# Cutting single matmuls of a split-precision product stream into 128-column pieces, and a last sub-layer in 256-column products

## The chip, the cores and the metric

The kernel runs on one core of one Trainium2 chip. The metric is the device time of one execution in microseconds; before the change it is 658.05 us, the median of three runs (657.58 to 658.54).

## What is computed

A two-layer decoder trunk on 256 tokens of width 1024, in float32. Layer 0 is a gated DeltaNet mixer followed by a squared-ReLU MLP, layer 1 a block attention (at 256 tokens it is plain causal softmax with ALiBi) followed by another such MLP. Every sub-layer is preceded by an RMSNorm, and one more stands at the end. Cut to what matters:

```python
for i in range(DEPTH):
    hn = rmsnorm(h, mix_norm_g[i])
    mix = gated_deltanet(hn, ...) if i % 2 == 0 else moba_layer(hn, ...)
    h = h + mix
    h = h + squared_relu_mlp(rmsnorm(h, mlp_norm_g[i]), mlp_w_up[i], mlp_w_down[i])
return rmsnorm(h, final_norm_g)
```

MLP: `square(relu(hn @ w_up)) @ w_down`, with 4096 hidden features.

## The kernel before

**Split products.** Each large weight product is made from three matmuls. A weight `w` and an activation `x` are each split into a high part and a rest (`wh`, `wl`, `xh`, `xl`, type fp32r), and `wh*xh + wh*xl + wl*xh` is summed in PSUM. `mm3` (lines 128 to 131) issues the three; the 128x128 weights are stationary and 256 tokens stream. In `natural` (lines 207 to 222) and in `mlp_last` the roles are turned: a 128x128 piece of the activation is stationary and up to 512 columns of weights stream. Every matmul brings its own load of the stationary side, so there are as many weight loads as matmuls. Below, a **split product** is one matmul of this kind; an **fp32 product** is a plain fp32 matmul or transpose (norm sums, attention scores, the recurrence).

**Weights.** They come as 200 units of 128x1024 from HBM in a fixed order. `unit()` hands out the next and prepares four ahead: SP issues the DMA, ScalarE makes `wh` (line 115), VectorE `wl` (line 116).

**Order of the work.** It is the program's order. Layer 0: the DeltaNet, in which split products of `pair` alternate with blocks of fp32 products by the hand-written string `ORDER`; `project_out("g")` (tiles `ps_g`, interleaved at its beginning with the last of the recurrence); MLP 0 in `mlp_up` (tiles `ps_up_m`, 16 calls of `pair`, 48 split products each) and `mlp` (`ps_dn_m`, 768). Layer 1: attention by the string `ATT` (tiles `ps_qk`, `ps_vn`, with fp32 blocks `s`, `ptp`, `pv` between), `project_out("a")` (`ps_a`, 192 split products), four transposes each for two token tiles (`hNt`), then `mlp_last`: 768 split products of `mlp_up` and the down product. The norm of an MLP is finished late: `nm.finish()` is called after the first `pair`, and issues four fp32 sums (`n_ps`) and two fp32 broadcasts (`n_pb`) among the split products of the first two pairs. Behind `n_pb` there is no fp32 product until the end of MLP 0 and the first pair of attention (`n_ps` of the next norm), and none until the end of the kernel in MLP 1.

**The last sub-layer.** `mlp_last` makes the down product in two halves of 512 output features. In each, for 8 groups of 4 hidden tiles and 2 token tiles `tt`, 12 split products run. Three of the four (half, tt) stream 512 columns into one PSUM bank, the last (half 1, tt 1) streams 256 columns at a time into two banks (`ps_last`, `ps_last_e`), so that the first 256 can be taken out earlier. `part`, `scaled` and `store` (lines 295 to 320) add, sum squares, scale and store.

Of the kernel before, what the change touches and what calls it, by code (L numbers as in the profile page):

```python
# [14 lines left out]
P = 128  # L15
T = 256
D = 1024
KT = D // P
H = 8
FF = 4 * D  # L20
NFF = FF // P
# [7 lines left out]
NLAST = 2  # L29
NTANH = 3  # L30
RS = 3.0 / 8
LASTCUT = 256
# [43 lines left out]
def trunk_kernel(ctx: ExitStack, tc: tile.TileContext, xT, wst, wba, par, con, selc, gfin, out):  # L76
    nc = tc.nc
# [8 lines left out]
    def bank(role, shape, name):  # L86
        tag = ROLE[role]
        return psum.tile(shape, F32, tag=tag, name=name, bufs=BANKS[tag])
# [32 lines left out]
    def unit():  # L121
        u = cur[0]
        cur[0] += 1
        for i in range(u, u + LEAD + 1):
            prep(i)
        return ring[u]

    def mm3(o, wh, wl, xh, xl, start, stop):
        nc.tensor.matmul(o, wh, xh, start=start, stop=False, skip_group_check=True)  # L129
        nc.tensor.matmul(o, wh, xl, start=False, stop=False, skip_group_check=True)  # L130
        nc.tensor.matmul(o, wl, xh, start=False, stop=stop, skip_group_check=True)  # L131

    def mm(o, l, r, start=True, stop=True):
        nc.tensor.matmul(o, l, r, start=start, stop=stop, skip_group_check=True)  # L134
# [56 lines left out]
            self.bc = small.tile([P, T], F32, tag="nbc", name=f"{self.name}_bc", bufs=2)  # L191
            nc.scalar.copy(self.bc, pb[:, :T])

    def pair(nm, name):

        ps = bank("acc", [P, 2, T], f"ps_{name}")
        for c in range(2):
            wh, wl = unit()
            for k in range(4):
                kt = 4 * c + k  # L200
                for n in range(2):
                    s = slice((k * 2 + n) * P, (k * 2 + n + 1) * P)
                    mm3(ps[:, n, :], wh[:, s], wl[:, s], nm.xh[:, kt, :], nm.xl[:, kt, :],
                        kt == 0 and n == 0, kt == KT - 1)
        return ps

    def natural(nm, name):
# [16 lines left out]
    def project_out(name, oh, ol, hin, nxt):  # L224

        pss = [bank("out" + "abcd"[i], [P, 2, T], f"ps_{name}_{i}") for i in range(4)]

        def piece(hd, n, w):
            s = slice(n * P, (n + 1) * P)
            mm3(pss[n // 2][:, n % 2, :], w[0][:, s], w[1][:, s], oh[:, hd, :], ol[:, hd, :],  # L230
                hd == 0 and n % 2 == 0, hd == H - 1)

        first = H - NLAST
        for hd in range(first):
            w = unit()
            for n in range(KT):
                piece(hd, n, w)
        w = [unit() for _ in range(first, H)]
        hout = act.tile([P, KT, T], F32, tag="h", name=f"h_{name}")
        for n in range(KT):  # L240
            for k in range(H - first):
                piece(first + k, n, w[k])
            if n % 2:
                i = n // 2
                nc.vector.tensor_add(hout[:, 2 * i:2 * i + 2, :], hin[:, 2 * i:2 * i + 2, :], pss[i])
                nxt.feed(hout, i)
        return hout

    def mlp_up(hp, name, nm):
        hp.tile([P, 336], F32, tag="fill", name=f"fill_{name}")  # L250
        hh = hp.tile([P, NFF, T], F32R, name=f"hh_{name}")
        hl = hp.tile([P, NFF, T], F32R, name=f"hl_{name}")
        for i in range(NFF // 2):
            ps = pair(nm, f"up_{name}_{i}")
            if i == 0:
                nm.finish()
            r1 = hp.tile([P, 2, T], F32, tag="r1", name=f"r1_{name}_{i}", bufs=2)
            nc.vector.scalar_tensor_tensor(r1, ps, 0.0, nm.bc[:, None, :].to_broadcast([P, 2, T]),
                                           op0=ALU.max, op1=ALU.mult)
            sq = hp.tile([P, 2, T], F32, tag="sq", name=f"sq_{name}_{i}", bufs=2)  # L260
            nc.scalar.activation(sq, r1, AF.Square)
            s = slice(2 * i, 2 * i + 2)
            nc.scalar.copy(hh[:, s, :], sq)
            nc.vector.tensor_sub(hl[:, s, :], sq, hh[:, s, :].bitcast(F32))
        return hh, hl
# [19 lines left out]
    def mlp_last(nm, hin):  # L285

        with tc.tile_pool(name="hid_last", bufs=1) as hp:
            hh, hl = mlp_up(hp, "m1", nm)
            gf = hp.tile([P, D], F32, name="gf")
            nc.sync.dma_start(gf, gfin)  # L290
            hg = hp.tile([P, 2, D], F32, name="hg")
            junk = hp.tile([P, 2, 512], F32, name="junk")
            ss = small.tile([P, 2, 3], F32, tag="ssf", name="ssf", bufs=1)

            def part(tt, a, b, k, o):

                f = slice(a, b)
                nc.vector.tensor_add(hin[:, tt, f], hin[:, tt, f], o)
                nc.scalar.activation(junk[:, tt, :b - a], hin[:, tt, f], AF.Square, accum_out=ss[:, tt, k:k + 1])

            def scaled(tt, a, b):
                nc.vector.scalar_tensor_tensor(hg[:, tt, a:b], hin[:, tt, a:b], RS, gf[:, a:b],
                                               op0=ALU.mult, op1=ALU.mult)

            def store(tt):
                so = small.tile([P, 1], F32, tag="sof", name=f"sof{tt}", bufs=2)
                if tt == 0:
                    nc.vector.tensor_scalar(so, ss[:, tt, 0:1], D * EPS, None, op0=ALU.add)
                else:
                    nc.vector.scalar_tensor_tensor(so, ss[:, tt, 0:1], D * EPS, ss[:, tt, 1:2],  # L310
                                                   op0=ALU.add, op1=ALU.add)
                ms = small.tile([P, 1], F32, tag="msf", name=f"msf{tt}", bufs=2)
                nc.vector.tensor_scalar(ms, ss[:, tt, 1 + tt:2 + tt], so, 1.0 / D, op0=ALU.add, op1=ALU.mult)
                r = rsqrt(ms, 1, f"fin{tt}")
                for a, b, q in ((0, DCUT, nc.sync), (DCUT, D, nc.scalar)):
                    if a == 0:
                        nc.vector.tensor_scalar(hg[:, tt, a:b], hg[:, tt, a:b], r, None, op0=ALU.mult)
                    else:
                        nc.scalar.activation(hg[:, tt, a:b], hg[:, tt, a:b], AF.Copy, scale=r)
                    q.dma_start(out[tt, :, a:b], hg[:, tt, a:b])  # L320

            for half in range(2):
                f0 = half * 512
                pss = [bank("acc", [P, 512], f"ps_last_{half}_{tt}") for tt in range(2)]
                pse = bank("pv0", [P, 512], f"ps_last_{half}_e")
                for c in range(0, NFF, 4):
                    w = [unit(), unit()]
                    for tt in range(2):
                        for a, b in ((0, LASTCUT), (LASTCUT, 512)) if half + tt == 2 else ((0, 512),):
                            o = pse[:, :b - a] if a else pss[tt][:, :b]  # L330
                            for k in range(4):
                                kt = c + k
                                wh, wl = w[k // 2]
                                s = slice(k % 2 * 512 + a, k % 2 * 512 + b)
                                xh, xl = hh[:, kt, tt * P:(tt + 1) * P], hl[:, kt, tt * P:(tt + 1) * P]
                                mm(o, xh, wh[:, s], kt == 0, False)
                                mm(o, xh, wl[:, s], False, False)
                                mm(o, xl, wh[:, s], False, kt == NFF - 1)
                            if c == NFF - 4:
                                part(tt, f0 + a, f0 + b, half + (a > 0), o)  # L340
                                scaled(tt, f0 + a, f0 + b)
                                if half == 1 and (tt == 0 or a):
                                    store(tt)
# [27 lines left out]
    with tc.tile_pool(name="gd", bufs=2) as gd:  # L371
# [349 lines left out]
        for tok in ORDER.split():  # L721
            c, n = tok[0], int(tok[1:] or 0)
# [33 lines left out]
        oh, ol = OH  # L756
        n1 = Norm("n1", G_MLP0)
        h1 = project_out("g", oh, ol, h0, n1)
    n2 = Norm("n2", G_MIX1)
    h2 = mlp("m0", n1, h1, n2)  # L760


    with tc.tile_pool(name="at", bufs=2) as at:
# [64 lines left out]
        for tok in ATT.split():  # L828
            {"q": do_qk, "s": do_soft, "t": do_pt, "V": do_vn, "p": do_pv}[tok[0]](int(tok[1:]))
        n3 = Norm("n3", G_MLP1)  # L830
        h3 = project_out("a", ah, al, h2, n3)
    hN = act.tile([P, 2, KT, P], F32, tag="h", name="hN")
    for tt in range(2):
# [124 lines left out]
```

## Time and profile before

| | |
|---|---|
| median of the runs | 658.05 us |
| the profiled execution | 658.23 us |
| its span, first to last instruction | 656.4 us |
| PE (TensorE matmul) busy | 643.4 us, 98% |
| PEld (weight load) busy | 605.2 us, 92% |
| DVE (VectorE), ACT (ScalarE) busy | 454.6 us (69%), 345.6 us (53%) |
| HBM read | 107.51 MB, 165 GB/s over the span |

Times are us from the start of the span. L130 is line 130 of the kernel. A matmul's shown duration is its latency: matmuls overlap in the array, so the time that one takes from the stream is the distance from its start to the next start, called its **pace** here.

### The profile page before, as it was taken

The page shows a single profiled execution, that of the slowest core. Times are in us where ns is not written, and L with a number is a line of the kernel's source. Part 1 is how long each engine was busy: PE and PEld are TensorE (multiplying, and loading weights), DVE is VectorE, ACT ScalarE, POOL GpSimd, SP SyncE. Part 2 cuts the span into 40 slices and gives each one's busy share as a digit, 9 for nine tenths or more (in the row PEclk, how much of TensorE's full clock was granted, in tenths as well). Part 3 has the DMA queues.
Part 4 walks back from the last instruction along what each step waited for, and adds up shares of the span by engine and source line. Part 5 has one row for each costly group of instructions (what it writes and reads, how often), then busy time and mean ns, then how long its engine had stood idle before and what let it go on. Part 6 is the DMA issues. An engine that isn't in the chain of part 4 may idle for free.

```text
span 656.4 us, 13349 instructions
## 1 busy us (share of the span) xinstructions
PE 643.4 (98%) x5454; PEld 605.2 (92%) x5454; DVE 454.6 (69%) x841; ACT 345.6 (53%) x570; POOL 4.0 (1%) x10
## 2 busy tenths in 40 slices
PE   8999999999999999999999999999999999999995
PEld 6999878979999999999999999889999999888994
DVE  5899998997897666645554668775976666545443
ACT  7689782553575555534443444543655555434331
POOL 1000000000000000000000000000000000000000
PEclk9999999999999999999999999999999999999998
DMA  8754151342555555565555555555365555556531
GB/s 268 240 171 154 36 192 68 103 126 65 187 168 193 187 176 189 187 193 190 179 182 190 184 169 161 165 157 170 119 224 191 185 178 190 171 188 186 190 129 65
DMA packets 32029, 109.42 MB, mean 167 GB/s; under 512 B 3552, under 2 KB 3936, under 8 KB 31968
## 3 DMA queue, kind: packets, MB, share of 16 engines
q1 hardware_dynamic: 31248, 107.71, 49.9%
q8 instruction: 43, 0.70, 0.4%
q10 hardware_dynamic: 720, 0.86, 0.4%
q14 instruction: 18, 0.15, 0.1%
HBM read 107.51 MB, written 1.05 MB: 165 GB/s over the span
## 4 chain that ended last, share of the span: by engine, by line
PE 86%; DVE 6%; DMA 4%; ACT 3%; issue 1%; DVEq 0%; ACTq 0%
PE ps_last L134 12%; PE ps_up_m L130 9%; PE ps_up_m L131 9%; PE ps_up_m L129 9%; PE ps_dn_m L130 5%; PE ps_dn_m L129 5%; PE ps_dn_m L131 5%; PE ps_vn L134 3%; DMA wf<-in_w 3%; PE ps_z L134 3%; DVE wl L116 2%; PE ps_qk L130 2%; PE ps_qk L131 2%; PE ps_qk L129 2%; PE kk L134 2%; PE ps_last_e L134 1%
## 5 line engine op out<-in xcount | busy, mean ns | idle before, releaser
L116 DVE TENSOR_TENSOR wl<-wf,wh 128x1024 fp32r<-128x1024 f32 (+1 forms) x208 | 244.8, 1182 | 144.9 <-ACT wh L115 144.5
L115 ACT CAST wh<-wf 128x1024 fp32r<-128x1024 f32 (+1 forms) x208 | 210.7, 1017 | 244.3 <-PE ps_up_m L130 65.4
L130 PE MATMUL ps_up_m<-n_l,wh 128*128 128x256 f32 x512 | 143.9, 281 | 0.2 <-DVE n_l L168 0.2
L131 PE MATMUL ps_up_m<-n_h,wl 128*128 128x256 f32 x512 | 144.0, 281 | 0.0
L129 PE MATMUL ps_up_m<-n_h,wh 128*128 128x256 f32 x512 | 143.8, 281 | 0.0
L129 PEld LDWEIGHTS ps_up_m<-n_h,wh 128*128 128x128 f32 x512 | 98.0, 192 | 0.0
L130 PEld LDWEIGHTS ps_up_m<-n_l,wh 128*128 128x128 f32 x512 | 96.2, 188 | 0.3 <-DVE n_l L168 0.3
L131 PEld LDWEIGHTS ps_up_m<-n_h,wl 128*128 128x128 f32 x512 | 96.1, 188 | 0.0
L129 PE MATMUL ps_dn_m<-hh_m,wh 128*128 128x256 f32 x256 | 71.9, 281 | 0.0
L130 PE MATMUL ps_dn_m<-hl_m,wh 128*128 128x256 f32 x256 | 71.9, 281 | 0.0
L131 PE MATMUL ps_dn_m<-hh_m,wl 128*128 128x256 f32 x256 | 71.9, 281 | 0.0
L129 PEld LDWEIGHTS ps_dn_m<-hh_m,wh 128*128 128x128 f32 x256 | 49.2, 192 | 0.0
L130 PEld LDWEIGHTS ps_dn_m<-hl_m,wh 128*128 128x128 f32 x256 | 48.1, 188 | 0.0
L131 PEld LDWEIGHTS ps_dn_m<-hh_m,wl 128*128 128x128 f32 x256 | 48.1, 188 | 0.0
L134 PE MATMUL ps_last<-wh,hl_m 128*128 128x512 f32 (+1 forms) x128 | 46.9, 366 | 0.0
L134 PE MATMUL ps_last<-wl,hh_m 128*128 128x512 f32 (+1 forms) x128 | 46.8, 366 | 0.0
L134 PE MATMUL ps_last<-wh,hh_m 128*128 128x512 f32 (+1 forms) x128 | 46.7, 365 | 0.0
L129 PE MATMUL ps_kq<-n_h,wh 128*128 128x256 f32 x128 | 36.5, 285 | 0.0
L129 PE MATMUL ps_qk<-n_h,wh 128*128 128x256 f32 x128 | 36.3, 283 | 0.0
L131 PE MATMUL ps_kq<-n_h,wl 128*128 128x256 f32 x128 | 36.0, 281 | 0.0
L130 PE MATMUL ps_kq<-n_l,wh 128*128 128x256 f32 x128 | 35.9, 280 | 0.0
L130 PE MATMUL ps_qk<-n_l,wh 128*128 128x256 f32 x128 | 35.7, 279 | 0.0
(278 smaller groups left out, 1254.3 us busy)
## 6 DMA issues: line engine op xcount, KB each, us to landing
wf<-in_w SPq DMA_DIRECT2D x192, 512.0 KB, 3.5
wf<-in_w SPq DMA_DIRECT2D x16, 256.0 KB, 3.9
h<-in_x SPq DMA_DIRECT2D x4, 256.0 KB, 6.5
gf<-in_g SPq DMA_DIRECT2D x1, 512.0 KB, 3.8
out<-hg SPq DMA_DIRECT2D x2, 256.0 KB, 2.1
out<-hg ACTq DMA_DIRECT2D x2, 256.0 KB, 2.5
sel<-in_sel SPq DMA_DIRECT2D x1, 448.0 KB, 4.7
cn<-in_con SPq DMA_DIRECT2D x1, 276.0 KB, 5.1
```

Source lines behind the costliest of these rows:

```text
L115: nc.scalar.copy(wh[:, s], wf[:, s])
L116: nc.vector.tensor_sub(wl[:, s], wf[:, s], wh[:, s].bitcast(F32))
L129: nc.tensor.matmul(o, wh, xh, start=start, stop=False, skip_group_check=True)
L130: nc.tensor.matmul(o, wh, xl, start=False, stop=False, skip_group_check=True)
L131: nc.tensor.matmul(o, wl, xh, start=False, stop=stop, skip_group_check=True)
L134: nc.tensor.matmul(o, l, r, start=start, stop=stop, skip_group_check=True)
```

## The change

`mm3` gets a flag `cut`: with it, the middle of its three matmuls (`wh*xl`) is issued as two matmuls of 128 columns each, with the same stationary side, which is loaded for each. The flag is set at ten places: in each of the two `project_out` at (head, n) = (2, 1), (5, 1) and (6, 1); in each of the two `mlp_up` in pairs 2 and 4, at the fifth `mm3` of the pair (kt 2, n 0). The last sub-layer streams 256 columns in all four (half, tt): the 288 products of 512 columns become 576 of 256. Both 256-column halves go to the same bank there, except for (half 1, tt 1), which is as before; `part` and `scaled` are called on the same columns as before. In each half one product (kt 1, tt 0, first 256 columns) is in two pieces of 128 columns: the eleventh and twelfth place.

```diff
-    def mm3(o, wh, wl, xh, xl, start, stop):
+    def mm3(o, wh, wl, xh, xl, start, stop, cut=False):
+
         nc.tensor.matmul(o, wh, xh, start=start, stop=False, skip_group_check=True)
-        nc.tensor.matmul(o, wh, xl, start=False, stop=False, skip_group_check=True)
+        for s in (slice(0, P), slice(P, T)) if cut else (slice(0, T),):
+            nc.tensor.matmul(o[:, s], wh, xl[:, s], start=False, stop=False, skip_group_check=True)
         nc.tensor.matmul(o, wl, xh, start=False, stop=stop, skip_group_check=True)
...
-    def pair(nm, name):
+    def pair(nm, name, cut=False):
...
-                        kt == 0 and n == 0, kt == KT - 1)
+                        kt == 0 and n == 0, kt == KT - 1, cut and (kt, n) == (2, 0))
...
+        first = H - NLAST
+
         def piece(hd, n, w):
...
-                hd == 0 and n % 2 == 0, hd == H - 1)
-
-        first = H - NLAST
+                hd == 0 and n % 2 == 0, hd == H - 1, (hd, n) in ((2, 1), (first - 1, 1), (first, 1)))
+
...
-            ps = pair(nm, f"up_{name}_{i}")
+            ps = pair(nm, f"up_{name}_{i}", i in (2, 4))
...
-                        for a, b in ((0, LASTCUT), (LASTCUT, 512)) if half + tt == 2 else ((0, 512),):
-                            o = pse[:, :b - a] if a else pss[tt][:, :b]
+                        for a, b in ((0, LASTCUT), (LASTCUT, 512)):
+                            own = half + tt == 2 and a > 0
+                            o = pse[:, :b - a] if own else pss[tt][:, a:b]
...
-                                mm(o, xh, wh[:, s], kt == 0, False)
-                                mm(o, xh, wl[:, s], False, False)
+                                mm(o, xh, wh[:, s], kt == 0 and (own or a == 0), False)
+                                if (kt, tt, a) == (1, 0, 0):
+                                    mm(o[:, :P], xh, wl[:, s.start:s.start + P], False, False)
+                                    mm(o[:, P:], xh, wl[:, s.start + P:s.stop], False, False)
+                                else:
+                                    mm(o, xh, wl[:, s], False, False)
                                 mm(o, xl, wh[:, s], False, kt == NFF - 1)
-                            if c == NFF - 4:
-                                part(tt, f0 + a, f0 + b, half + (a > 0), o)
+                            if c == NFF - 4 and (a or half + tt == 2):
+                                if half + tt < 2:
+                                    a, o = 0, pss[tt]
+                                part(tt, f0 + a, f0 + b, half + (1 if own else 0), o)
```

## Rows read from the trace of the kernel before

**Rows 1.** The page, parts 1 and 2: PE, and its granted clock.

```profile
PE 643.4 (98%) x5454; PEld 605.2 (92%) x5454; DVE 454.6 (69%) x841; ACT 345.6 (53%) x570; POOL 4.0 (1%) x10
...
PEclk9999999999999999999999999999999999999998
```

**Rows 2.** Stretches of split products alone: length, PE busy (matmuls), PEclk, DMA share, GB/s.

```profile
171.20:180.90 9.70, 9.70 (x88) 1.00 0.61 211
193.75:272.78 79.03, 79.03 (x673) 1.00 0.56 188
272.90:363.23 90.33, 90.33 (x769) 1.00 0.56 187
377.60:393.20 15.60, 15.60 (x140) 1.00 0.51 171
394.30:399.90 5.60, 5.60 (x50) 1.00 0.47 155
401.10:406.30 5.20, 5.20 (x48) 1.00 0.46 157
407.10:412.60 5.50, 5.50 (x49) 1.00 0.60 194
448.00:466.00 18.00, 18.00 (x161) 1.00 0.64 201
480.93:559.95 79.02, 79.02 (x673) 1.00 0.58 191
```

**Rows 3.** Timeline of PE where the fp32 products of MLP 0's norm end.

```profile
192.13 0.60 PE L134 MATMUL n_pb<-cn,n_col 128*128 128x128 f32 x4
...
192.49 0.36 PE L131 MATMUL ps_up_m<-n_h,wl 128*128 128x256 f32 x1
...
192.69 0.28 PE L129 MATMUL ps_up_m<-n_h,wh 128*128 128x256 f32 x1
...
192.81 0.28 PE L130 MATMUL ps_up_m<-n_l,wh 128*128 128x256 f32 x1
```

**Rows 4.** Timeline of PE: a stall inside a stream of split products.

```profile
183.67 0.39 PE L129 MATMUL ps_up_m<-n_h,wh 128*128 128x256 f32 x2
184.21 0.38 PE L130 MATMUL ps_up_m<-n_l,wh 128*128 128x256 f32 x1 [0.15 <-DVE n_l L168]
```

**Rows 5.** Timeline of PE in the last sub-layer: where the column count changes, and its last product.

```profile
607.68 0.28 PE L134 MATMUL ps_last<-wh,hh_m 128*128 128x256 f32 x1
...
610.50 0.40 PE L134 MATMUL ps_last<-wh,hh_m 128*128 128x512 f32 x1
...
613.26 0.28 PE L134 MATMUL ps_last<-wh,hh_m 128*128 128x256 f32 x1
...
614.62 0.28 PE L134 MATMUL ps_last_e<-wh,hh_m 128*128 128x256 f32 x1
...
648.67 0.28 PE L134 MATMUL ps_last_e<-wh,hl_m 128*128 128x256 f32 x1
```

**Rows 6.** Timeline of PE: from the first cuts of the MLPs to the stretches' ends.

```profile
195.40 0.28 PE L131 MATMUL ps_up_m<-n_h,wl 128*128 128x256 f32 x1
...
369.01 0.61 PE L134 MATMUL n_ps<-ones,n_acc 128*128 128x1 f32 x5
...
482.57 0.28 PE L131 MATMUL ps_up_m<-n_h,wl 128*128 128x256 f32 x1
...
560.07 0.40 PE L134 MATMUL ps_last<-wh,hh_m 128*128 128x512 f32 x1
```

**Rows 7.** Timeline of PE: six transposes of 128 columns, and what follows.

```profile
438.93 0.82 PE L803 MATMUL ptp<-cn,pr 128*128 128x128 f32 x6
439.59 0.82 PE L134 MATMUL pv<-pt,vn 128*128 128x256 f32 x4
```

**Rows 8.** Groups by shape: fp32 scores of 128 columns (8 products in the code).

```profile
L134 PE MATMUL s<-qk 128*128 128x128 f32 x16 | 3.1, 273 | 0.0
```

**Rows 9.** MLP 0's up product: PE, PEld, DVE, ACT, POOL busy, PEclk, DMA share, GB/s.

```profile
193.75:272.78 79.03, 79.03 (x673) 79.03 (x672) 54.02 (x58) 46.43 (x58) 0.00 (x0) 1.00 0.56 188
```

## Prediction

> **What bounds the kernel now.** I read the page first. PE is busy 98% of the span, in nearly every one of the 40 slices, at the full granted clock until the tail [rows 1]. So there are no waits to remove: the time is the number of matmuls times the pace at which they follow one another. A matmul's shown duration (0.28 us) is no help for that; I counted starts in the windows and the timeline.
>
> The windows of pure 256-column split products show the one thing that matters here: **the same instruction runs at two paces.** A window counts every matmul that touches it, so two are taken off for those begun before. MLP 0's up product is 671 matmuls in 79.03 us, its down product 767 in 90.33 us, MLP 1's up product 671 in 79.02 us: 117.8 ns each. Attention at 377.6 has 138 in 15.60 us and the output projection at 448 has 159 in 18.00 us: 113.0 and 113.2 ns [rows 2]. In the last sub-layer 12 products go from 613.26 to 614.62, so 113.3 ns [rows 5]. I use 113.3 (fast) and 117.8 (slow), 4.45 ns or 3.8% apart.
>
> The pace does not come from the instructions or from traffic. The four attention stretches between 394 and 413 us run the same lines on the same tiles, by counts slow, fast, slow (117, 113, 117), the one at 377.6 fast; the DMA share is 0.51 and 0.46 in two fast ones, 0.47 and 0.60 in two slow ones, 0.64 in the fast projection [rows 2]. It comes from history: each stretch stands behind a block of fp32 products, the first split products behind it are irregular (200 ns from 192.49 to 192.69, then 120 [rows 3]), and then one pace is held without a change until the next fp32 block or stall. MLP 0 is unlucky: behind the norm's fp32 broadcast it comes out slow, and has no fp32 product again before 369.01, so it stays slow for 173.6 us. MLP 1 likewise.
>
> **Can a cut change the pace?** No 128-column split product exists in the trace, so this is the step that I have to judge. The nearest thing is a change of the column count inside a stream without any fp32 product, in the last sub-layer. From 560.07 to 607.68 there are 204 products of 512 columns (192 of half 0 and the first 12 of half 1) at 233.4 ns, two slow paces; from 607.68 to 610.50, 24 of 256 columns at 117.5, still slow; then 12 of 512 from 610.50 to 613.26 at 230; and from 613.26 on 256 columns run at 113.3 [rows 5, 6]. So of three changes of width (at 560.07, 607.68 and 610.50 us) one turned slow into fast, with no fp32 product near. From 613.26 to the end the width changes 12 more times and the pace never falls back: 35.5 us to the last product, where 168 of 113.3 and 72 of 229 give 35.5. Fast is thus the pace that disturbances of this kind leave alone, slow the one that they can end. Only a stall shows the contrary: PE waits 0.15 us at 184.21 for the activations [rows 4], and the products behind it start 0.12 us apart in place of 0.11. A cut is two changes of width, and each long stretch has two cuts. I take it that MLP 0 and MLP 1 are fast from their first cut on.
>
> **The sum.**
> 1. MLP 0: the first cut is the product before 195.40. From there to 369.01 (rest of the up product, the down product, the first attention pair) the slow stream takes 173.61 us, 1474 products [rows 6]. At 113.3 it takes 6.55 us less. The second cut is 96 products later; should only that one act, 0.43 us of it is lost.
> 2. MLP 1: from 482.57 to 560.07, 77.50 us [rows 6], 658 products: 2.93 us less.
> 3. Last sub-layer: from 560.07 to 648.78 (the last start plus 0.11) it takes 88.71 us [rows 5, 6]. All in 256 columns it is 768 products, 87.04 us at the fast pace: 1.67 us less. It is entered from the fast stream of MLP 1, and has a cut in each half.
> 4. The twelve cuts. Each adds one matmul and one load of 128 stationary columns. Six transposes, with 128 columns on both sides, take 0.66 us from 438.93 to 439.59, 110 ns each [rows 7], nearly as long as 256 columns of a split product, so I take it that with so few columns the load sets the pace. Two pieces take 220 ns in place of 113 to 118: 105 ns per cut, 1.26 us in all. From below, pieces at half a fast product (57 ns) cost nothing: 0. From above, a piece as dear as an fp32 product of 128 columns, for which the trace has two records [rows 8], so 220 ns per piece, and behind it the irregular start (87 ns over a normal product [rows 3]): 440 + 87 - 118 = 409 ns, 4.9 us for twelve. I take 1.26, because the transposes have the pieces' column count and one record each.
> 5. The six cuts in the two output projections: the windows at 171.2 and 448 us, where five of them fall, are fast already [rows 2], so I book no gain, only the price above. If such a cut made it slow, some 100 products until the next fp32 block would lose 0.45 us. The other short stretches behind fp32 blocks may come out the other way in attention, where each is some 48 products, 0.2 us: 0.7 us either way for all.
> 6. Nothing for weights: a unit feeds 24 products, 2.72 us at the fast pace, which asks for 193 GB/s; the fast projection had 201 GB/s without a wait [rows 2]. In MLP 0's up product DVE is busy 54.0 and ACT 46.4 of 79.0 us [rows 9]; in 3 us less DVE reaches 71%, which still lies beside PE. If that cover went, PE would wait for `wl` and could lose at most what it gained.
> 7. Nothing for taking results out: the adds, squares and stores work on the same columns behind the same last product, beside the next (half, tt) on PE; the tail behind the last product is the same. The 288 extra loads in the last sub-layer lie beside the matmuls, as in the 256-column streams before.
>
> Sum: -6.55 - 2.93 - 1.67 + 1.26 = -9.89 us. The profiled execution took 658.23, 0.18 above the median, and 1.8 above its span, which stays: 648.3 for it, **648.2 us** against the median of 658.05.
>
> One rule speaks against the change. The rows give 233.4 and about 229 ns for 512 columns, and 226.6 for two fast products of 256 [rows 5, 6], so the narrower form is the cheaper one when fast. The Trainium skill, "TensorE: Matmul & The Clock Gate", section "Back-to-back issue gap", has the columns at 2.4 GHz plus about 2.5 ns for each matmul, with no second pace: then 288 more products and 12 more pieces are pure loss, by an estimate from its figures 0.8 us. Rows 2 do not agree with one gap per shape.
>
> **The rivals.**
> - *The slow pace survives (slower, 15%).* What holds the pace through 1497 products (192.69 to 369.01 at 117.8 ns) may also hold through two short pieces, as it held through two of the three changes of width above. Then MLP 0 and 1 win nothing, the cuts cost 1.26, and the last sub-layer, no longer shaken by 512-column products, runs 768 at 117.8, 90.47 us, 1.76 more: 658.05 + 3.0 = 661.1 us. It decides if neither MLP turns. Against it: the one turn seen without an fp32 product, and that behind fp32 blocks the fast pace comes about as often as the slow one [rows 2], so that the slow one is no rule of this stream. The page named above would come to this side too, since for it there is no pace to win.
> - *One of the two MLPs stays slow (14%).* If a cut draws the pace anew rather than mending it, the second cut can undo the first. MLP 1 slow with a fast last sub-layer: 651.1; MLP 0 slow: 654.7 us. For it: the stall that made a fast stream slow [rows 4].
> - *Dear pieces (4%).* The cuts act but cost their upper bound: 648.2 + 3.6 = 651.8 us.
> - *No difference (3%).* Both MLPs stay slow and the last sub-layer is fast: 658.05 + 1.26 - 1.67 = 657.6 us.
>
> **How the numbers follow.** The forecast, both MLPs and the last sub-layer fast, has 64%; its own range is 646.3 (free cuts and lucky attention) to 649.6 (second cuts needed, unlucky attention). The range for 8 in 10 takes in the second and third case up to 654.7 and leaves out the last and the slower one: 646.3 to 655.0. About 0.2%, 1.3 us, is what a measurement of this kernel can tell from no change. Faster: 64 + 14 + 4 = 82%; same: 3%; slower: 15%.
>
> **What the profile after would show.** Right: the windows that answer to 193.75, 272.90 and 480.93 hold their 671 and 767 products in 76.0 and 86.9 us; the last sub-layer takes 87.2 us with its cuts; the pieces start about 0.11 us apart; DMA in the MLPs is near 195 GB/s and PE has no new wait. Wrong: 0.118 us between starts behind both cuts of an MLP (the slow pace survives), fast between the cuts and slow behind the second (a new draw each time), pieces 0.2 us apart (dear), or idle PE before `wl` (step 6).

## The result and the profile after

The kernel after takes 650.33 us (median of four runs, 649.47 to 651.13) against 657.82 us before: a ratio of 0.9885, interval 0.9867 to 0.9902, 7.5 us less. The forecast was 648.2 in a range of 646.3 to 655.0; for the case that came, all long streams fast, its own bounds were 646.3 to 649.6, and 650.33 lies above them. The profiled execution took 651.13 us, its span 649.3.

PE on the page after, and the windows of pure split products that answer to [rows 2]; columns as there:

```profile
PE 634.4 (98%) x5754; PEld 608.5 (94%) x5754; DVE 453.7 (70%) x841; ACT 345.1 (53%) x570; POOL 4.0 (1%) x10
```

```profile
208.79:271.90 63.11, 63.11 (x559) 1.00 0.61 196
272.03:358.95 86.92, 86.92 (x769) 1.00 0.61 194
372.50:389.20 16.70, 16.70 (x145) 1.00 0.54 181
491.20:554.30 63.10, 63.10 (x559) 1.00 0.63 198
598.80:641.00 42.20, 42.20 (x374) 1.00 0.41 129
```

With two taken off for those begun before, both up products and the down product now run at 113.3 ns, and so does the last sub-layer. The attention stretch at 372.5, fast before, came out slow (143 in 16.70 us is 116.8 by this short count; its starts are 117.8 apart). So the long slow stretches are gone. But this profile does not show that a cut did it. The timeline of PE from the norm's broadcast to the first cut of MLP 0 in the kernel after:

```profile
194.97 0.68 PE L136 MATMUL n_pb<-cn,n_col 128*128 128x128 f32 x4 [0.24 <-DVE n_col L189]
195.40 0.37 PE L133 MATMUL ps_up_m<-n_h,wl 128*128 128x256 f32 x1
...
195.96 0.28 PE L130 MATMUL ps_up_m<-n_h,wh 128*128 128x256 f32 x1
...
196.98 0.28 PE L130 MATMUL ps_up_m<-n_h,wh 128*128 128x256 f32 x1
197.09 0.33 PE L132 MATMUL ps_up_m<-n_l,wh 128*128 128x128 f32 x2
197.26 0.33 PE L133 MATMUL ps_up_m<-n_h,wl 128*128 128x256 f32 x1
197.43 0.28 PE L130 MATMUL ps_up_m<-n_h,wh 128*128 128x256 f32 x1
```

Nine products go from 195.96 to 196.98, 113.3 ns each: the stream was fast **before** the cut at 197.09. MLP 1 is the same: its starts are 113 to 114 ns apart ahead of its first cut at 479.44. Another thing is new here: PE waits 0.24 us for `n_col` ahead of the broadcast, which it did not before [rows 3]. The view of who waited for whom on PE (us in total, times, longest), cut to three waits that the kernel before lacks or has shorter:

```profile
PE n_pb L136 <- DVE n_col L189: 0.6, 2, 0.4
PE ps_up_m L130 <- ACT n_h L169: 0.5, 1, 0.5
PE hNt L847 <- DVE h_a L248: 0.5, 1, 0.5
```

So after the result three theories stood: a cut ends the slow pace and leaves the fast one alone (mending); a cut draws the pace anew; the cuts are bystanders, and the waits in front of the broadcasts brought the fast pace.

### The profile page after: what moved, and what is told of

Its sections match the earlier page's. It is cut to its first block, busy times and chain, and to the rows that moved or that the text cites. A ratio compares the mean times of both kernels' runs of the same rounds, so it can differ in the third digit from the quotient of the medians.

```text
span 649.3 us, 13944 instructions
## 1 busy us (share of the span) xinstructions
PE 634.4 (98%) x5754; PEld 608.5 (94%) x5754; DVE 453.7 (70%) x841; ACT 345.1 (53%) x570; POOL 4.0 (1%) x10
## 4 chain that ended last, share of the span: by engine, by line
PE 85%; DVE 5%; ACT 5%; DMA 4%; issue 1%; ACTq 0%; DVEq 0%
PE ps_last L136 12%; PE ps_up_m L132 8%; PE ps_up_m L133 8%; PE ps_up_m L130 8%; PE ps_dn_m L133 4%; PE ps_dn_m L132 4%; PE ps_dn_m L130 4%; PE ps_vn L136 3%; DMA wf<-in_w 3%; PE ps_z L136 3%; DVE wl L116 2%; PE ps_qk L132 2%; PE ps_qk L133 2%; PE ps_qk L130 2%; ACT wh L115 2%; PE kk L136 2%
## 5 line engine op out<-in xcount | busy, mean ns | idle before, releaser
L130 PE MATMUL ps_up_m<-n_h,wh 128*128 128x256 f32 x512 | 141.6, 277 | 0.5 <-ACT n_h L169 0.5
L132 PE MATMUL ps_up_m<-n_l,wh 128*128 128x256 f32 (+1 forms) x516 | 141.9, 276 | 0.0
L133 PE MATMUL ps_up_m<-n_h,wl 128*128 128x256 f32 x512 | 141.8, 277 | 0.0
L130 PEld LDWEIGHTS ps_up_m<-n_h,wh 128*128 128x128 f32 x512 | 96.1, 188 | 0.7 <-ACT n_h L169 0.7
L136 PE MATMUL ps_last<-wl,hh_m 128*128 128x256 f32 x226 | 61.9, 276 | 0.0
L136 PE MATMUL ps_last<-wh,hl_m 128*128 128x256 f32 x224 | 61.9, 276 | 0.0
L136 PE MATMUL ps_last<-wh,hh_m 128*128 128x256 f32 x224 | 61.8, 276 | 0.0
L136 PEld LDWEIGHTS ps_last<-wl,hh_m 128*128 128x128 f32 x226 | 42.3, 188 | 0.0
L136 PEld LDWEIGHTS ps_last<-wh,hh_m 128*128 128x128 f32 x224 | 42.1, 188 | 0.0
L136 PEld LDWEIGHTS ps_last<-wh,hl_m 128*128 128x128 f32 x224 | 42.0, 188 | 0.0
```

The costliest lines, as they stand in the source:

```text
L132: nc.tensor.matmul(o[:, s], wh, xl[:, s], start=False, stop=False, skip_group_check=True)
```

## The experiments

Edits are against the kernel after unless said, cut to the lines that matter. "Slow" and "fast" mean the two paces, 117.8 and 113.3 ns between starts. Windows shorter than 4 us hold too few matmuls to tell them apart, so there the distance between starts decides.

### The four cuts of the up products alone

```diff
-                hd == 0 and n % 2 == 0, hd == H - 1, (hd, n) in ((2, 1), (first - 1, 1), (first, 1)))
+                hd == 0 and n % 2 == 0, hd == H - 1, False)
```

and the last sub-layer as before.

> The kernel of before with the four cuts of the two up products alone. Three theories. Mending: a cut ends the slow pace and leaves the fast one alone; then whatever pace stands behind the norm's broadcast, everything behind the first cut of each MLP starts 113.3 ns apart, and the time is 657.8 - 6.55 - 2.93 + 4 x 0.126 (the price of a cut in the profile after) = 648.8 us, or 647 to 650 with other short stretches. New draw: each cut draws the pace again, so each MLP is fast in about half of the cases: 648.8, 651.7, 655.3 or 658.3 us. Bystander: the profile after was fast already behind the broadcast, at 195.96 and 478.87 us, ahead of the first cuts, because PE had waited there; the cuts only cost: with the pace of before 658.3 us, and no change of pace at a cut.

Measured: 648.98 us (four executions, 648.18 to 651.38), ratio 0.984 (0.976 to 0.992). Timeline of PE at the first cut, then windows:

```profile
194.69 0.28 PE L132 MATMUL ps_up_m<-n_l,wh 128*128 128x256 f32 x1
...
195.28 0.28 PE L130 MATMUL ps_up_m<-n_h,wh 128*128 128x256 f32 x1
195.40 0.33 PE L132 MATMUL ps_up_m<-n_l,wh 128*128 128x128 f32 x2
195.57 0.33 PE L133 MATMUL ps_up_m<-n_h,wl 128*128 128x256 f32 x1
195.74 0.28 PE L130 MATMUL ps_up_m<-n_h,wh 128*128 128x256 f32 x1
195.86 0.28 PE L132 MATMUL ps_up_m<-n_l,wh 128*128 128x256 f32 x1
195.97 0.28 PE L133 MATMUL ps_up_m<-n_h,wl 128*128 128x256 f32 x1
```

```profile
207.10:269.90 62.80, 62.80 (x557) 1.00 0.61 194
270.40:357.20 86.80, 86.80 (x768) 1.00 0.61 194
```

Behind the broadcast the stream is slow (six products from 194.69 to the cut at 195.40, 118 ns each); three starts behind the cut it is at 113.3 and stays there for the 555 and 766 products of the two windows. PE did not wait before the broadcast (115 ns between starts). MLP 1 turned in the same way at its first cut. That is mending, at the expected time; the bystander theory falls.

### The kernel after without these four

```diff
-            ps = pair(nm, f"up_{name}_{i}", i in (2, 4))
+            ps = pair(nm, f"up_{name}_{i}")
```

> The kernel after without the four cuts of the up products; those of the projections and of the last sub-layer stay. Mending: the pace behind each broadcast is what the fp32 block leaves and is held to the next fp32 block or, in MLP 1, to the cut in the last sub-layer; if the broadcasts leave it fast as in the profile after, 650.3 - 0.5 = 649.8 us; if slow, 650.3 - 0.5 + 6.5 for MLP 0 and + 2.9 for MLP 1, up to 659.2 us, with the last sub-layer turning fast at its first cut. Bystander: 649.8 us if the waits are as in the profile after, and a slow MLP 1 would leave the last sub-layer slow across its cuts.

Measured: ten executions in three groups: 648.6 to 650.8 us (five), 656.3 and 656.7 (two), 661.9 to 663.3 (three). The steps between them fit step 1 of the prediction (6.5 for MLP 0) and a slow MLP 1 with a slow last sub-layer behind it (2.9 and 3.4). Only the longest execution, 663.31, was profiled; which stream was slow in the others is inferred from these steps. Its windows:

```profile
195.80:274.70 78.90, 78.90 (x673) 1.00 0.59 187
...
485.00:563.10 78.10, 78.10 (x665) 1.00 0.59 187
564.10:608.90 44.80, 44.80 (x382) 1.00 0.55 182
609.50:653.50 44.00, 44.00 (x376) 1.00 0.38 122
```

All are slow. So behind a broadcast that PE waits for, the pace differs from execution to execution, and without cuts it is kept. And two cuts in the last sub-layer, at 563.7 and 609.0, ended nothing: mending failed there.

### The last sub-layer alone

```diff
-            ps = pair(nm, f"up_{name}_{i}", i in (2, 4))
+            ps = pair(nm, f"up_{name}_{i}")
...
-                                if (kt, tt, a) == (1, 0, 0):
+                                if False:
```

and no cut in the projections.

> The kernel of before with the last sub-layer in 256 columns and no cut at all. All theories: no fp32 product and no change of width stands between MLP 1's broadcast and the end, so one pace holds for the up product's rest and the last sub-layer. If MLP 1 is slow as before: the last sub-layer takes 768 x 117.8 = 90.5 us and the kernel 657.8 + 1.8 = 659.6 us. If MLP 1 comes out fast: 87.0 us, and 657.8 - 2.9 - 1.7 = 653.2 us.

Measured: 660.03 us (ten executions, 658.25 to 661.44), ratio 1.0014 (0.9996 to 1.0032): no gain, and both MLPs and the last sub-layer slow from end to end in the profile. The expected 659.6 holds. In the kernel before, the last sub-layer came to the fast pace among changes of width [rows 5]; 256 columns throughout take that away, and pay only when MLP 1 hands over a fast stream.

### A cut in every pair

```diff
-                        kt == 0 and n == 0, kt == KT - 1, cut and (kt, n) == (2, 0))
+                        kt == 0 and n == 0, kt == KT - 1, (kt, n) == (2, 0))
```

with the projections uncut and the last sub-layer as before.

> The kernel of before with a cut in every call of the pair function (52 of them: mixers and both up products), at the thirteenth split product of each, to count what a cut does to a pace that stands before it. Mending: all stretches that are slow ahead of a cut are fast behind it, and all that are fast stay so; both MLPs fast to their ends. New draw: about half of the slow ones turn, and as many of the fast ones turn slow. Bystander: no pace changes at a cut. The cuts cost 48 x 0.126 = 6.0 us more than four; by mending the time is about 654 to 655 us.

Measured: 656.56 us, one execution. One of its cuts, in attention, in windows on either side of the cut at 395.74:

```profile
394.50:395.70 1.20, 1.20 (x12) 1.00 0.96 362
396.20:399.60 3.40, 3.40 (x33) 1.00 0.31 92
```

Starts are 117.8 apart ahead of it and 113.4 behind it. The count covers all cuts into 128 + 128 with the weights stationary, in the ten profiles of this study that have them; left out are those whose two pieces stand apart in the program's order, and six behind which PE stalls within a dozen products. **23 of 23 slow streams turned fast, 70 of 70 fast ones stayed fast.** A new draw at each cut is refuted.

### Cuts at other places of the last sub-layer

```diff
-                                if (kt, tt, a) == (1, 0, 0):
+                                if half == 0 and (kt, tt, a) in ((1, 0, 0), (6, 0, 0), (10, 1, 256), (16, 0, 0), (22, 0, 0)):
```

no other cut.

> The last sub-layer in 256 columns, no cut elsewhere, so that it is entered slow (as in each of the runs with last only). In the run without the up products' cuts two cuts of the last sub-layer, each at hidden tile 1, left the pace slow. Here five cuts stand in half 0, in this order: hidden tile 1 (as in the change; the next product is the first on a new weight unit and waits on semaphores), tile 6 (in the middle of a unit), tile 10 (second token tile, second 256 columns, middle of a unit), tiles 16 and 22. Theory of the wait: the semaphore waits behind tile 1 undo the cut, so tile 6 turns the pace fast, and everything behind it stays at 113.3 ns: last sub-layer about 87.4 us plus cuts. Theory of the form: with the activation stationary a cut does not mend at any place; the last sub-layer is slow to the end, 90.5 us plus five cuts, 0.5 us.

Measured: 660.36 us, one execution. Windows behind the first, the second and the last of the five cuts:

```profile
561.00:566.50 5.50, 5.50 (x49) 1.00 0.54 179
567.00:576.50 9.50, 9.50 (x83) 1.00 0.50 172
...
590.00:609.00 19.00, 19.00 (x164) 1.00 0.55 169
```

Each is slow (47, 81 and 162 products: 117 each), also where no semaphore wait follows. The theory of the wait falls.

### Other matmuls, other pieces in the last sub-layer

```diff
+            CUTS = {2: {0: 128}, 6: {2: 128}, 10: {1: 64}, 14: {0: 128, 1: 128, 2: 128}, 18: {1: 128}, 19: {1: 128}, 22: {1: 192}}
```

(hidden tile: matmul of the three: columns of the first piece; half 0, first token tile and columns).

> The last sub-layer in 256 columns, entered slow, no cut elsewhere; in its first token tile and first 256 columns stand, in order: the first matmul in two pieces (hidden tile 2), the third (tile 6), the second as 64 + 192 (tile 10), all three in two (tile 14), the second of two neighbouring tiles (18, 19), the second as 192 + 64 (tile 22). In the run before, five cuts of the second into 128 + 128 left the pace at 117.8. If the stream with the activation stationary can be mended by pieces at all, one of these turns it to 113.3 and the rest stays fast (87.0 us against 90.5 for the sub-layer); if the form cannot, all is slow, 658 + 1.8 + 8 x 0.11 = 660.7 us.

Measured: 659.68 us, one execution. Windows: MLP 1, behind the first cut, ahead of the last and behind it.

```profile
480.50:560.00 79.50, 79.50 (x677) 1.00 0.60 192
561.00:566.30 5.30, 5.30 (x49) 1.00 0.54 182
...
584.00:588.80 4.80, 4.80 (x44) 1.00 0.64 204
589.20:609.00 19.80, 19.80 (x170) 1.00 0.52 167
```

Neither expectation held whole. With the *first* matmul of a triple in two pieces the slow stream turned fast (starts 0.113 apart behind 560.61), the next four kinds of pieces left it fast, and 192 + 64 columns of the second turned it slow again for good (168 in 19.80 us). Each of these turns was seen once. They suggest that in this form, with the activation stationary, it depends on which matmul is cut and how.

### Which matmul of the triple, weights stationary

```diff
-            ps = pair(nm, f"up_{name}_{i}", i in (2, 4))
+            ps = pair(nm, f"up_{name}_{i}", {"m0": {2: 0, 5: 2, 8: 1}, "m1": {2: 2, 5: 0, 8: 1}}[name].get(i))
```

(pair: index of the matmul of the three that is cut, 0 to 2; `mm3` is changed to cut that one). Last sub-layer in 256 columns, no other cut.

> Which of the three matmuls may be cut. The last sub-layer in 256 columns without cuts; in the up products one cut each of pairs 2, 5 and 8, at the same place: in MLP 0 first the first matmul (wh*xh), then the third (wl*xh), then the second (wh*xl, as in the change); in MLP 1 third, first, second. The fp32 blocks keep the places of before, so both MLPs should come out slow behind the broadcast. If any change of width mends, both turn fast at pair 2. If only the second matmul does, both turn at pair 8, and the two lose 2 x 288 x 4.45 ns = 2.6 us against the run with two cuts: about 650 us. If the first mends and the third does not, MLP 0 turns at pair 2 and MLP 1 at pair 5.

Measured: 647.93 us, one execution. Timeline ahead of the first cut of MLP 0 (the first matmul, at 194.87) and of MLP 1 (the third, at 476.49), and the window behind each:

```profile
194.28 0.28 PE L133 MATMUL ps_up_m<-n_l,wh 128*128 128x256 f32 x1
...
194.87 0.33 PE L133 MATMUL ps_up_m<-n_h,wh 128*128 128x128 f32 x2
...
475.90 0.28 PE L133 MATMUL ps_up_m<-n_h,wh 128*128 128x256 f32 x1
...
476.49 0.34 PE L133 MATMUL ps_up_m<-n_h,wl 128*128 128x128 f32 x2
```

```profile
195.70:211.40 15.70, 15.70 (x141) 1.00 0.62 187
477.20:492.50 15.30, 15.30 (x138) 1.00 0.64 198
```

Ahead of each cut five products take 0.59 us, 118 ns each; behind it the windows hold 139 and 136, 113 and 112.5. Both turned within seven starts. The second matmul turned the stream in 21 cases, the first and the third in one each: with the weights stationary any of the three can be cut.

### Uneven pieces in the MLPs

```diff
-            ps = pair(nm, f"up_{name}_{i}", i in (2, 4))
+            ps = pair(nm, f"up_{name}_{i}", {2: P, 4: 192}.get(i, 0))
```

(pair: columns of the first piece, which `mm3` now takes). Last sub-layer in 256 columns, no other cut.

> The run with two cuts, and in pair 4 of each MLP the second matmul of the same place in 192 + 64 columns. In the last sub-layer such pieces were followed by the slow pace although the stream was fast. If it is the sizes of the pieces that leave a stream slow, both MLPs are fast from pair 2 to pair 4 and slow behind it: MLP 0 with 1378 products (562 up, 768 down, 48 attention) loses 6.1 us, MLP 1 with 562 loses 2.5, the last sub-layer, entered slow, 3.4: 647.1 + 12.0 + 0.2 = 659.3 us, with nothing else changed. If the turn belongs to the last sub-layer's form, the MLPs stay fast: 647.4 us.

Measured: 648.43 us (four executions, 647.47 to 649.06), ratio 0.985 (0.983 to 0.986). Windows behind the 192 + 64 of MLP 0 and of MLP 1:

```profile
207.00:270.00 63.00, 63.00 (x558) 1.00 0.62 193
...
488.00:550.90 62.90, 62.90 (x557) 1.00 0.62 194
```

The streams stayed fast: 556 and 555 products at 113.3 ns. So the turn to slow, seen once, belongs to the last sub-layer's form and not to these sizes as such.

### Two cuts, four cuts, and the kernel after beside them

```diff
-            ps = pair(nm, f"up_{name}_{i}", i in (2, 4))
+            ps = pair(nm, f"up_{name}_{i}", i == 2)
```

and no cut elsewhere; the last sub-layer in 256 columns.

> The change with one cut in each MLP (pair 2) and none elsewhere; the last sub-layer in 256 columns, without cuts. By the mending theory these two cuts do all that the twelve do: both MLPs fast from pair 2 on and, with no fp32 product between, the last sub-layer fast too. Against the run with the four cuts of the up products: 2 x 0.126 less for cuts, and the last sub-layer 0.65 less (87.69 to 87.04 us): about 0.9 us below it, 648.1 us. Order theory: without the projections' cuts the fp32 blocks keep the places that they have before, and the waits of PE for the norm and the transposes that the profile after shows do not come: 1 to 2 us below the kernel after. If instead a single cut does not do it each time, some executions are 3 to 11 us longer.

> The same with two more cuts, where a long stretch can come out slow: (head 5, n 1) in the first output projection (about 100 products behind it) and attention pair 2 (130 behind it). Mending: each gains 0.45 to 0.58 us less 0.10 when its stretch is slow, and costs 0.126 when it is fast, so between 0.25 us longer and 0.8 us shorter than with two cuts: 647.3 to 648.4 us. In the profile neither stretch is slow behind its cut.

> The kernel after, beside the two above on the same chip. Order theory: both are 1 to 2 us below it, of which ten cuts explain 10 x 0.12 = 1.2 and waits the rest. Mending: it is never in a long slow stretch, so all executions lie within 2 us; its times depend on the draw in the short stretches alone.

Measured, on one chip: two cuts 647.12 us (646.55 to 647.18), ratio 0.9825 (0.9809 to 0.9841); four cuts 647.88 (646.95 to 648.19), 0.9837 (0.9820 to 0.9855); the kernel after 650.31 (649.09 to 652.43), 0.9877 (0.9857 to 0.9898). Two cuts are 3.2 us below the kernel after. In this second profile of the kernel after, MLP 0 came out slow behind its broadcast, and its first cut, at 196.25, ended that:

```profile
195.19 0.28 PE L132 MATMUL ps_up_m<-n_l,wh 128*128 128x256 f32 x1
...
196.25 0.34 PE L132 MATMUL ps_up_m<-n_l,wh 128*128 128x128 f32 x2
...
196.95 0.28 PE L130 MATMUL ps_up_m<-n_h,wh 128*128 128x256 f32 x1
...
197.52 0.28 PE L133 MATMUL ps_up_m<-n_h,wl 128*128 128x256 f32 x1
```

Ahead of the cut nine products take 1.06 us (118 ns each), from 196.95 on five take 0.57 (114). Windows with two cuts, behind the first of them and in the last sub-layer; ahead of each cut the starts are 118 ns apart there:

```profile
194.70:268.90 74.20, 74.20 (x657) 1.00 0.63 196
...
550.10:639.00 88.90, 87.17 (x770) 1.00 0.48 155
```

The last sub-layer, 768 products without a cut, takes 87.0 us because it is entered fast; entered slow, in the run with the last sub-layer alone, the same products take 90.5. With four cuts both added ones turned a slow stream fast in the profile, yet the median does not show a gain. Such short stretches are worth 0.4 to 0.6 us less the price; that they are slow only in some executions would explain it, but was not shown.

### The projections' cuts put back

```diff
-            ps = pair(nm, f"up_{name}_{i}", i in (2, 4))
+            ps = pair(nm, f"up_{name}_{i}", i == 2)
...
-                                if (kt, tt, a) == (1, 0, 0):
+                                if False:
```

The six cuts of the output projections stay.

> The run with two cuts (647.1 us), with the six cuts of the output projections put back. The order in which the program issues its matmuls changes by them: in MLP 0 the norm's sums stand behind 58 split products in place of 49. Order theory: PE waits for the norm's activations, the broadcasts and the transposes again, about 2 us as in the profile after: 647.1 + 6 x 0.126 + 2.2 = 650.0 us. Price theory: the cuts cost only their own time: 647.9 us.

Measured: 649.67 us (six executions, 648.47 to 650.60), ratio 0.987 (0.985 to 0.989): 2.55 us above two cuts (measured on another chip, where the kernel before differs by 0.24), where the cuts' own time explains 6 x 0.126 = 0.76. PE's waits, the three that the run with two cuts does not have:

```profile
PE n_pb L136 <- DVE n_col L189: 0.9, 3, 0.4
...
PE ps_up_m L130 <- ACT n_h L169: 0.5, 1, 0.5
PE hNt L847 <- DVE h_a L248: 0.5, 1, 0.5
```

One of the three waits for `n_col` stands ahead of MLP 0 and its 0.3 us does not belong here. The stages of the two profiles tell it better. From MLP 0's first product to its cut it takes 15.13 us against 14.08 with two cuts, from MLP 1's to its cut 16.14 against 15.32: 1.9 us more. The second projection, with its three cuts, takes 23.46 against 23.08. Every other stage behind the first projection agrees within 0.02, and the part ahead of MLP 0 is 0.23 shorter in spite of three cuts. In the profiles' order of matmuls the norm's sums stand behind 58 split products of MLP 0 here and in the kernel after, behind 49 in the kernel before and in each run with uncut projections; MLP 1's transposes and broadcast are moved too. So the six extra matmuls changed the order in which the program is laid out, and that order waits. The order theory holds.

## Why the prediction was right

**What bounds the kernel, and the two paces: right.** The gains by stage are the booked ones. The rows of the kernel after's timeline at the stages' bounds, beside 197.09 above:

```profile
364.51 0.28 PE L136 MATMUL n_ps<-ones,n_acc 128*128 128x1 f32 x2
...
479.44 0.33 PE L132 MATMUL ps_up_m<-n_l,wh 128*128 128x128 f32 x2
...
554.38 0.28 PE L136 MATMUL ps_last<-wh,hh_m 128*128 128x256 f32 x1
...
641.53 0.28 PE L136 MATMUL ps_last_e<-wh,hl_m 128*128 128x256 f32 x1
```

From the first cut of MLP 0 to the attention's first norm block the kernel before takes 173.73 us (195.28, the start before 195.40, to 369.01 [rows 6]), the one after 167.42: 6.31 less, which is the 6.55 of step 1 less two cuts. MLP 1 from its first cut to the last sub-layer: 77.61 (482.46, the start before 482.57, to 560.07) and 74.94, 2.67 less, step 2 less two cuts. The last sub-layer, with 0.11 for the last product, takes 87.26 us against 88.71 [rows 5, 6]: 1.45 less, step 3 less two cuts. Together 10.43.

**That a cut mends: right for the MLPs, but the result alone did not show it**, since both streams were fast ahead of their cuts. The run with four cuts and the second profile of the kernel after showed it, and the count of 23 and 70 made it a rule of this form. The argument from the changes of width in the last sub-layer held only in its conclusion, which was luck: that stream has another form, in which the same cut ended the slow pace in none of seven cases, and in which one kind of piece ended the fast one.

**Step 3, "has a cut in each half": wrong as a safeguard.** What made the last sub-layer fast was the stream that entered it.

**Step 4, the price: right in size, by luck.** I took 105 ns per cut, because I had each piece take 110. In a fast stream the first piece takes 57 ns and the second 113, the next product 170, the three behind it 117.5: 692 ns where five fast products (the cut one and those four) take 567, so 126. The pieces are cheaper than I thought, and more than half of the price falls on the products behind them.

**Step 5 is the term that was mis-sized.** I booked no gain and only the price for the projections' cuts, and expected no new wait on PE. The price was right, but the cuts also moved the fp32 blocks in PE's order, and PE now waits at the norm of each MLP and at the transposes: 1.8 us by the run that puts them back. With the dearer price (12 x 0.021 = 0.25) that makes 2.05, and 648.2 becomes 650.25, close to the measured 650.33. It lies in the range that I gave only because that range left room for two of the rivals.

The two profiles, 7.1 us apart, add up as well. From the span's start to MLP 0 the kernel after is 1.1 us behind, from there to the cut 0.7, in attention and its projection 0.7, from there to MLP 1's cut 0.8: 3.3 us, and 10.4 less 3.3 is 7.1. Of the 3.3 the six cuts are 0.8, and the stretches from each MLP's first product to its first cut, with their waits, 1.5. Attention adds 0.3, in which the stretch at 372.5, drawn slow, costs 0.64. The last 0.7 lies ahead of MLP 0, where the profiles scatter between 179.9 us (the run above, with three cuts there) and 182.3 (the run with the last sub-layer alone, without any), so that nothing ties it to the change.

**Step 6: right.** The down product moved 194 GB/s at the fast pace without a wait.

**The rivals.** The slow pace's survival is refuted for the MLPs. It is what happens in the last sub-layer. A new draw at each cut is refuted by the count, and dear pieces by the 126 ns. The gap rule of the Trainium skill, "TensorE: Matmul & The Clock Gate", "Back-to-back issue gap", which that section gives for a single matmul by itself, would have made the run with two cuts no faster than before. That run is 11.0 us faster with 290 more matmuls, so here the measurement decides.

## What to carry to other kernels

Where PE is never idle, measure the distance between starts, stretch by stretch, and compare it for one and the same instruction: a second pace, kept for hundreds of matmuls, does not show in PE's busy share (98% before and after). One matmul in two pieces of 128 columns behind a block of another kind ended the slow pace here, with the weights stationary, for 0.13 us; place it only where a long stream follows, and check in the order of the instructions that the addition moved nothing else. When a result agrees with a forecast, look whether the named cause was at work before believing it: here it took a run with the cuts alone.

## What the runs showed that was not expected

**The slow pace of the kernel before was no chance.** The prediction called MLP 0 unlucky; the runs say otherwise. In the fourteen profiles PE goes from the last split product to a broadcast of an MLP's norm without a wait (115 ns) 19 times, and the stream behind is slow each time. Where it waits (271 to 653 ns between starts), it is fast in five of nine. So where PE did not wait there, the stream always came out slow, and in the order of the kernel after it comes out either way. Why the wait matters was not tested.

**The form counts.** With the weights stationary, 128 + 128 columns of any of the three matmuls ended the slow pace. With the activation stationary, the second matmul in 128 + 128 never did (seven of seven), the first did once, and 192 + 64 columns of the second once turned a fast stream slow. What in the streams makes the two paces, and why the forms differ, stays open: the trace shows when each matmul and load starts, and no run here separated the operands' places in memory from their roles. Nor did a run add a matmul of full width, so it is not shown whether the narrow pieces or the one more matmul with its load end the slow pace.
